# Four blocks on x without its 1/rms, key searches held back once, products given precedence, and a last block in two halves of tokens

## The chip, the cores and the metric

The kernel runs on one core of one Trainium2 chip. The metric is the device time of one execution in microseconds. Three runs of the kernel before gave 3128.99, 3129.6 and 3132.29 us, so the median is 3129.6.

## The reference, cut to what matters

Two transformer blocks run one after the other on 512 tokens of 1024 features, in float32. What the change touches:

```python
# first block
h = rmsnorm(x, norm1_g)                 # x * rsqrt(mean(x * x) + eps) * g
z = h @ w_in + b_in                     # 42 blocks of 128 columns
glu_val, glu_gate, q, k, v, g_conv, g_attn = split(z)
conv_out = conformer_conv(glu_val, glu_gate, ...)   # 31 taps over time
...
# peer: scores against keys, the best 16 of 128 in each half, then experts
q = (h2 @ w_pq).reshape(B, S, 8, 2, 128)
s_top, i_top = top_k(einsum("bshcd,hcnd->bshcn", q, sub_keys), 16)
...
# second block: swiglu, a mixer with two kinds of attention, swiglu, then
hn = rms_norm(h, ple_norm)
h = h + sigmoid(hn @ ple_w_gate) * (p @ ple_w_proj)
return rms_norm(h, final_norm)
```

## The kernel before, in words

Activations lie transposed: eight tiles of 128 features by 512 tokens, `x[0]` to `x[7]`. A product of a weight matrix with them is cut into blocks of 128 output columns. `block` (L213) loads one block's weights (512 KB for 1024 rows), splits them, and issues for each of the eight tiles the three products of `three` (L208): high half of the weights by high half of the activation, high by low, low by high, which together give float32 accuracy. The split of weights is `split` (L189): a cast on ACT (L190) gives the high half `wh`, a subtraction on DVE (L191) the low half `wl`. `wr`, `wh` and `wl` have three buffers each, so weights come up to three blocks ahead; their loads are issued on SP's queue. All products accumulate in eight PSUM banks (`ps`, L139); a bank is free again when its reader is done.

A norm is applied late where that is possible: the products take x times the gain, and their result is multiplied by 1/rms (`self.rstd`), as in `plain` of the mixer (L1051, the product on DVE at L1055). In the first block it is not so: `block1` (L382) squares x (L403, L404), sums over features with products by a column of ones (`col_mean`, L263), takes the root in small steps on DVE (`rsqrt`, L250), spreads it over 128 partitions by four transposes (`bcast`, L274) and a copy (L282), and only then multiplies x by it (L416) and splits the result into `hs`, which all 42 blocks of `w_in` read. Ahead of these stand eight small projections of the embedding `p` (`project`, L389), each copied by ACT (L395) and stored by a DMA that ACT issues (L396). Between them and block 0 stands also the product of `bias_table` (L340), whose result is stored to `rbd`.

The order of instructions on each engine and queue is made ahead of the run by a planner, which takes the instruction of lowest rank among those that it thinks ready; rank is the order in the program, and `high_priority(n)` puts instructions n places forward. Each engine and queue then works strictly in that order. Beside that the kernel spreads work by hand. `later` puts small pieces with a cost into a queue, and `run` (called by `block` with `self.rate`) takes pieces up to a budget: in block1 3.9 units after each block, at 0.65 for each of the 8 x 31 taps of the convolution (L455), which is six taps a block; in peer 4.5 units, at 1.0 for each search `best_keys` (L670), which has two maxima of eight with their places and one replacement. What is left of the searches after the last query block (`pending`, L702) is taken up in the expert stage at 2.2 units a block. `step` advances generators that stand one block back, and `lanes` with `pace` do the same inside the mixer's blocks.

In peer each of 16 query blocks ends with a product by 1/rms on DVE (L687), after which PE makes the scores (L691). Then x's normalized tiles `hn` are split (L704) and 128 expert blocks of 384 tokens follow (L905).

In the mixer the lanes `chosen` and `decays` run beside the blocks of the keys. `choose` makes scores of 128 queries with products at L1160, and searches their best 256 with L1171 and L1172 on DVE.

`tail` (L1445) makes eight blocks of `ple_w_gate`. Behind each follow a product by 1/rms (L1455), a sigmoid on ACT, a product, a sum into x, a square on ACT and a sum of squares (L300). After the last one come the column sums, the root, the broadcast with its copy, and eight last products (L1465), each stored.

Of the kernel before, what the change touches and what calls it, by code (L numbers as in the profile page):

```python
# [10 lines left out]
F32 = mybir.dt.float32  # L11
BF16 = mybir.dt.bfloat16
F32R = mybir.dt.float32r
# [3 lines left out]
AF = mybir.ActivationFunctionType  # L17
OP = mybir.AluOpType
# [4 lines left out]
S = 512  # L23
D = 1024
KD = D // 128
NT = S // 128
# [7 lines left out]
PH = 8  # L34
# [75 lines left out]
class Build:  # L110
    def __init__(self, ctx, tc, a, out):
# [5 lines left out]
        self.offset = 90  # L117
        self.early, self.soon = 160, 90
        self.pad = 3.0
# [183 lines left out]
    def setup(self):  # L303
# [20 lines left out]
        for i in range(4):  # L324
            s = slice(i * 512, (i + 1) * 512)
            self.load(wp[0][:, s], a["ple_w_proj"][:, s])
            self.split(wp[1][:, s], wp[2][:, s], wp[0][:, s])
        self.embedding = ph, wp
        table = sb.tile([128, -(-(NVEC + NCONST) // 32) * 32], F32, name="table")
        self.vecs, self.consts = table[:, :NVEC], table[:, NVEC:NVEC + NCONST]  # L330
        self.load(self.vecs, a["vecs"])
        self.x = []
        for m in range(KD):
            x = self.t("x", S, KD)
            self.load(x, a["x"][m])
            self.x.append(x)
        self.load(self.consts, a["consts"])
        self.ident = self.cst("ident")
# [43 lines left out]
    def block1(self):  # L382
# [14 lines left out]

        for m in range(3):
            project(m)
        accs = []  # L400
        for m in range(0, KD, 2):
            acc, q = (self.t("sq", S, 8, pool=self.ple) for _ in range(2))
            A.activation(acc, x[m], AF.Square)  # L403
            A.activation(q, x[m + 1], AF.Square)  # L404
            V.tensor_add(acc, acc, q)
            accs.append(acc)
        for m in range(3, 6):
            project(m)
        r = self.rsqrt(self.col_mean(accs, D, 1.0 / D), NT)
        for m in range(6, KD):  # L410
            project(m)
        rstd = self.bcast(r)
        hs = []
        for m in range(KD):
# [4 lines left out]
            hs.append((H, L))  # L419
        self.close_pool()  # L420

        b1 = self.ctx_pool("b1")
        c = lambda dt=F32: self.t("c", S, 26, dt, pool=b1)
        few = b1.tile([128, 128], F32, name="few")
# [7 lines left out]
        def gated(j, dst):  # L432

            A.activation(dst, self.block(a["w_in"][j], KD, hs), AF.Tanh, bias=hb[:, j:j + 1], scale=0.5)

# [3 lines left out]
        def glu(m):  # L439
            pv = self.block(a["w_in"][2 * m], KD, hs)  # L440
            v = self.tmp()
# [40 lines left out]
        kT, vtok = c(), c()  # L482
        qT = [b1.tile([128, 4, S], F32, name=f"q{i}") for i in range(2)]

# [154 lines left out]
    def peer(self, hs):  # L639
# [40 lines left out]
        for j in range(2 * PH):  # L680
            key = self.t("key", NKEY, 4, pool=hn_pool)
            self.load(key, a["keys"][j])
            p = self.block(a["w_peer_q"][j], KD, hs)

# [359 lines left out]
    def mixer(self, hs):  # L1044
# [6 lines left out]
        def plain(j, dst, rest=None):  # L1051
            p = self.block(win[j], KD, hs)

            def scale():
                V.tensor_mul(dst, p, self.rstd)  # L1055
                if rest:
                    rest()

            self.when(scale)
            return dst  # L1060
# [384 lines left out]
    def tail(self, hs):  # L1445
        nc, V, A, a, x = self.nc, self.V, self.A, self.a, self.x
        acc = self.t("acc", S, 2)
        for m in range(KD):
            pr = self.tmp()
            self.load(pr, self.prd[m])  # L1450
            p = self.block(a["ple_w_gate"][m], KD, hs)

            def rest(m=m, p=p, pr=pr):
                g = self.tmp()
                V.tensor_mul(g, p, self.rstd)  # L1455
                A.activation(g, g, AF.Sigmoid)
                V.tensor_mul(g, g, pr)
                V.tensor_add(x[m], x[m], g)
                self.sumsq(m, acc, x[m])

            self.when(rest)
        r = self.rsqrt(self.col_mean([acc], D, 1.0 / D), NT)
        rstd = self.bcast(r)
        for m in range(KD):
# [104 lines left out]
```

## Time and profile before

| what | value |
|---|---|
| median of three runs | 3129.6 us |
| the profiled execution | 3130.86 us |
| its span, first to last instruction | 3129.1 us |
| PE (products) busy | 3073.2 us, 98% |
| PEld (weight loads) busy | 2690.7 us, 86% |
| DVE busy | 2157.2 us, 69% |
| ACT busy | 1333.5 us, 43% |
| POOL busy | 304.1 us, 10% |
| mean granted TensorE clock | 0.992 |

The profile is of one execution. Times in its rows are microseconds from the span's start. A row of the timeline has the start, the duration, the engine, the line, the operation, what is written and read, and how many instructions are merged in it; in brackets stands the idle time of the engine before it and who ended that. PE is TensorE, PEld its weight loads, DVE VectorE, ACT ScalarE, SPq and ACTq the queues of SyncE and ScalarE that issue DMAs. Products are pipelined and their ends are modelled, so PE counts as busy from the first to the last of a dense row of them.

### The profile page before, as it was taken

Reading aid. Unit: us, or ns where it says so; the run is one execution under the profiler, and the core shown is the slowest. Engines: PE = TensorE matmul, PEld = TensorE weight load, DVE = VectorE, ACT = ScalarE, POOL = GpSimd, SP = SyncE. Lnnn points to the kernel's source line nnn. Section 1 sums busy time; section 2 is a strip of 40 time slices with the busy share of each in tenths; the row PEclk is TensorE's granted clock in tenths of the full one; section 3 lists DMA queues with packets and bytes.
Section 4 is the critical chain, followed back from the end, with each engine's and each line's share of the span. In section 5 each row is a group of like instructions: output and inputs, shape, how many; then the busy total and the mean of one; then the engine's idle time right before and its main releaser. Section 6 shows DMA issues by size and latency. Waiting matters only on the chain.

```text
span 3129.1 us, 41898 instructions
## 1 busy us (share of the span) xinstructions
PE 3073.2 (98%) x15557; PEld 2690.7 (86%) x15557; DVE 2157.2 (69%) x4086; ACT 1333.5 (43%) x2330; POOL 304.1 (10%) x266
## 2 busy tenths in 40 slices
PE   8999999999999999999999999999999999999997
PEld 6776678899999999999999988887688877888886
DVE  5998677999667766888888764433977655544435
ACT  4246543347888733333333433223433354332222
POOL 0000000011223233222222000000000000000000
PEclk9999999999999999999999999999999999999999
DMA  6321122266889999999999422233223333322332
GB/s 175 94 79 58 53 94 90 92 206 235 312 308 336 322 370 357 368 354 360 349 361 340 157 98 95 94 119 110 68 85 99 124 114 116 103 96 94 96 99 95
DMA packets 203796, 561.07 MB, mean 179 GB/s; under 512 B 20856, under 2 KB 82552, under 8 KB 200520
## 3 DMA queue, kind: packets, MB, share of 16 engines
q1 hardware_dynamic: 140208, 365.66, 34.2%
q0 software_dynamic: 37008, 134.53, 11.8%
q10 hardware_dynamic: 26376, 58.20, 5.2%
q8 instruction: 122, 2.00, 0.3%
q14 instruction: 82, 0.67, 0.1%
HBM read 494.58 MB, written 64.48 MB: 179 GB/s over the span
## 4 chain that ended last, share of the span: by engine, by line
PE 80%; DVE 14%; DMA 3%; ACT 2%; issue 1%; SPq 0%; ACTq 0%; DVEq 0%
PE ps L211 70%; DVE c L455 3%; DVE wl L191 3%; PE ps L834 2%; PE ps L1204 1%; DMA wr<-in_peer_u_dram 1%; DVE topi L676 1%; PE ps L565 1%; PE ps L527 1%; PE ps L1241 1%; DVE top L675 1%; PE ps L1359 1%; DMA tmp<-in_positions_dram 1%; PE ps L556 1%; DVE tk L745 1%
## 5 line engine op out<-in xcount | busy, mean ns | idle before, releaser
L190 ACT CAST wh<-wr 128x1024 fp32r<-128x1024 f32 (+1 forms) x560 | 584.8, 1044 | 1442.3 <-PE ps L211 784.5
L211 PE MATMUL ps<-hH,wh 128*128 128x512 f32 (+1 forms) x2816 | 1063.9, 378 | 5.9 <-ACT hH L190 2.6
L211 PE MATMUL ps<-hH,wl 128*128 128x512 f32 (+1 forms) x2816 | 1047.7, 372 | 10.0 <-DVE wl L191 9.8
L211 PE MATMUL ps<-hL,wh 128*128 128x512 f32 (+1 forms) x2816 | 1047.1, 372 | 0.3
L191 DVE TENSOR_TENSOR wl<-wr,wh 128x1024 fp32r<-128x1024 f32 (+1 forms) x560 | 679.6, 1214 | 338.6 <-ACT wh L190 308.1
L211 PEld LDWEIGHTS ps<-hH,wl 128*128 128x128 f32 x2816 | 531.0, 189 | 87.1 <-DVE wl L191 14.5
L211 PEld LDWEIGHTS ps<-hH,wh 128*128 128x128 f32 x2816 | 530.9, 189 | 83.9 <-issue 6.8
L211 PEld LDWEIGHTS ps<-hL,wh 128*128 128x128 f32 x2816 | 531.8, 189 | 72.9 <-issue 2.6
L211 PE MATMUL ps<-aH,wl 128*128 128x384 f32 (+1 forms) x1376 | 479.0, 348 | 0.0
L211 PE MATMUL ps<-aH,wh 128*128 128x384 f32 (+1 forms) x1376 | 478.9, 348 | 0.0
L211 PE MATMUL ps<-aL,wh 128*128 128x384 f32 (+1 forms) x1376 | 478.9, 348 | 0.0
L211 PEld LDWEIGHTS ps<-aL,wh 128*128 128x128 f32 x1376 | 258.3, 188 | 13.8
L211 PEld LDWEIGHTS ps<-aH,wl 128*128 128x128 f32 x1376 | 258.3, 188 | 13.7
L211 PEld LDWEIGHTS ps<-aH,wh 128*128 128x128 f32 x1376 | 258.3, 188 | 13.6
L860 POOL DMA_INDIRECT row<-in_peer_rows_dram,rows x128 | 161.2, 1259 | 1081.3 <-DVE tk L745 664.7
L860 POOL DMA_INDIRECT row<-in_peer_v_dram,rows x128 | 139.8, 1092 | 354.0 <-DVE acct L872 339.6
L455 DVE SCALAR_TENSOR_TENSOR c<-up,cw,c 128x512 f32<-128x512 f32 x240 | 171.4, 744 | 0.5
L872 DVE SCALAR_TENSOR_TENSOR acct<-row,dots,acct 128x1024 f32<-128x1024 f32 x127 | 162.3, 1278 | 0.0
L865 DVE CUSTOM_DVE_ANT_0 row<-row,htok 128x1024 f32<-128x1024 f32 x128 | 154.5, 1219 | 9.2 <-DMA row<-in_peer_rows_dram,rows 7.3
L211 PE MATMUL ps<-c,wh 128*128 128x512 f32 x384 | 126.2, 409 | 0.0
L1017 DVE TENSOR_TENSOR tmp<-ps,rstd 128x512 f32<-128x512 f32 x44 | 30.4, 691 | 129.8 <-PE ps L211 129.8
L821 DVE TENSOR_TENSOR ohr<-table,trip 128x512 f32<-128x512 f32 x96 | 65.1, 689 | 77.3 <-PE ps L834 73.3
(315 smaller groups left out, 2964.8 us busy)
## 6 DMA issues: line engine op xcount, KB each, us to landing
wr<-in_peer_u_dram SPq DMA_DIRECT2D x128, 512.0 KB
wr<-in_peer_v_dram SPq DMA_DIRECT2D x128, 512.0 KB
wr<-in_ffn_w_in_dram SPq DMA_DIRECT2D x88, 512.0 KB
gd<-tmp ACTq DMA_DIRECT2D x128, 192.0 KB
wd<-wb ACTq DMA_DIRECT2D x24, 1024.0 KB
g<-gd SPq DMA_DIRECT2D x128, 192.0 KB
wr<-in_mix_w_in_dram SPq DMA_DIRECT2D x46, 512.0 KB
wr<-in_w_in_dram SPq DMA_DIRECT2D x42, 512.0 KB
```

Source lines behind the costliest of these rows:

```text
L190: self.A.copy(H, src)
L191: return self.V.tensor_sub(L, src, H.bitcast(F32)).ins
L211: self.T.matmul(ps, l, r, start=first and i == 0, stop=last and i == 2)
L455: V.scalar_tensor_tensor(y, u[:, w:w + S], cw[:, i:i + 1], y, op0=OP.mult, op1=OP.add)
L527: T.matmul(pq[:, j * nk:(j + 1) * nk], qT[ga][P, i * 2 + j, tok], kT[P, k0:k0 + nk], start=True, stop=True)
L556: T.transpose(pt[:, i * 128:i * 128 + 128], sc[i // 2][:, o:o + 128], self.ident)
L565: T.matmul(po[P, :], vtok[:, kb + kv * 64:kb + kv * 64 + 64], pTs[b], start=b == 0, stop=b == nb - 1)
L821: V.tensor_tensor(r4, iota[:, None, :].to_broadcast([128, 4, 128]), trip[:, 128 + o:132 + o, None].to_broadcast([128, 4, 128]), op=OP.is_e ...
L834: T.matmul(pw[:, k * 128:k * 128 + 128], l4[:, k], r4[:, k], start=True, stop=True)
L860: G.indirect_dma_start(out=g, out_offset=None, in_=table, in_offset=bass.IndirectOffsetOnAxis(ap=rows[:, i * NF + j:i * NF + j + 1], axis=0))
L865: V.tensor_tensor_reduce(out=g, in0=g, in1=htok, scale=1.0, scalar=0.0, op0=OP.mult, op1=OP.add, accum_out=dots[:, j:j + 1])
L872: V.scalar_tensor_tensor(acct, g, dots[:, j:j + 1], acct, op0=OP.mult, op1=OP.add)
```

## The change

It has five parts.

1. The projections all come first. The weights of block 0 of `w_in` are loaded and split in `setup`, ahead of `vecs` and `x`. The tiles of x times the gain, without 1/rms, are split into high and low halves `raw` (60 places forward); high halves lie in the tiles that later hold the queries, low halves in tiles of the attention's scores. Blocks 0 to 3 multiply `raw`, and `first_block` multiplies their results by 1/rms; blocks from 4 on use `hs` as before. The constants are loaded after block 0. Squares use the buffers `tmp`, of which there are seven, in place of eight of their own. As blocks 2 and 3 are made before the taps are queued, they no longer carry any.
2. In peer `self.rate` is set to 0 ahead of the last query block.
3. In the mixer the product L1055 gets 40 places of precedence.
4. In the tail the last block is made in two halves of 256 tokens, with the steps behind it on each half, and its squares lie in a tile of their own that the column sums read beside the sum of the others.
5. The last products read the broadcast in PSUM, without the copy.

```diff
--- before.py
+++ after.py
@@ -115,7 +115,7 @@
         self.waiting, self.rstd = None, None
         self.lanes, self.credit, self.budget = [], 0, 0.8
         self.offset = 90
-        self.early, self.soon = 160, 90
+        self.early, self.soon, self.first = 160, 90, 60
         self.pad = 3.0
 
         self.on_act = lambda t: (0, 1) if t == 2 else (0, 1, 2)
@@ -326,6 +326,9 @@
             self.load(wp[0][:, s], a["ple_w_proj"][:, s])
             self.split(wp[1][:, s], wp[2][:, s], wp[0][:, s])
         self.embedding = ph, wp
+        keep, self.offset = self.offset, 0
+        self.first_weights = self.weights(a["w_in"][0], KD)
+        self.offset = keep
         table = sb.tile([128, -(-(NVEC + NCONST) // 32) * 32], F32, name="table")
         self.vecs, self.consts = table[:, :NVEC], table[:, NVEC:NVEC + NCONST]
         self.load(self.vecs, a["vecs"])
@@ -334,7 +337,6 @@
             x = self.t("x", S, KD)
             self.load(x, a["x"][m])
             self.x.append(x)
-        self.load(self.consts, a["consts"])
         self.ident = self.cst("ident")
 
     def bias_table(self):
@@ -395,21 +397,38 @@
             A.copy(r, p)
             nc.scalar.dma_start(self.prd[m], r)
 
-        for m in range(3):
+        for m in range(KD):
             project(m)
+        self.close_pool()
+
+        b1 = self.ctx_pool("b1")
+        c = lambda dt=F32: self.t("c", S, 26, dt, pool=b1)
+        quad = lambda i, dt=F32: b1.tile([128, 4, S], dt, name=f"q{i}", tag=f"q{i}", bufs=1)
+
+
+        high = [quad(i, F32R) for i in range(2)]
+        raw = []
+        with self.tc.high_priority(self.first):
+            for m in range(KD):
+                H = high[m // 4][:, m % 4, :]
+                L = self.t("sc", S, 6, F32R, pool=b1) if m < 6 else self.t("acc", S, 2, F32R)
+                A.activation(H, x[m], AF.Copy, scale=self.vec("norm1_g", m))
+                V.scalar_tensor_tensor(L, x[m], self.vec("norm1_g", m), H.bitcast(F32), op0=OP.mult, op1=OP.subtract)
+                raw.append((H, L))
+        ahead = [self.ps()]
+        for k in range(KD):
+            self.three(ahead[0], self.first_weights[k], raw[k], k == 0, k == KD - 1)
+        self.load(self.consts, a["consts"])
         accs = []
         for m in range(0, KD, 2):
-            acc, q = (self.t("sq", S, 8, pool=self.ple) for _ in range(2))
+            acc, q = self.tmp(), self.tmp()
             A.activation(acc, x[m], AF.Square)
             A.activation(q, x[m + 1], AF.Square)
             V.tensor_add(acc, acc, q)
             accs.append(acc)
-        for m in range(3, 6):
-            project(m)
-        r = self.rsqrt(self.col_mean(accs, D, 1.0 / D), NT)
-        for m in range(6, KD):
-            project(m)
-        rstd = self.bcast(r)
+        mean = self.col_mean(accs, D, 1.0 / D)
+        ahead.append(self.block(a["w_in"][1], KD, raw))
+        rstd = self.bcast(self.rsqrt(mean, NT))
         hs = []
         for m in range(KD):
             h = self.tmp()
@@ -417,10 +436,16 @@
             H, L = self.t("hH", S, 8, F32R), self.t("hL", S, 8, F32R)
             self.split(H, L, h)
             hs.append((H, L))
-        self.close_pool()
-
-        b1 = self.ctx_pool("b1")
-        c = lambda dt=F32: self.t("c", S, 26, dt, pool=b1)
+        ahead += [self.block(a["w_in"][j], KD, raw) for j in range(2, 4)]
+
+        def first_block(j):
+
+            if not ahead:
+                return self.block(a["w_in"][j], KD, hs)
+            r = self.tmp()
+            V.tensor_mul(r, ahead.pop(0), rstd)
+            return r
+
         few = b1.tile([128, 128], F32, name="few")
         hb, lnb, lng, sink = few[:, 0:42], few[:, 42:50], few[:, 50:58], few[:, 58:74]
         V.tensor_scalar(hb, self.vecs[:, VCOL["b_in"]:VCOL["b_in"] + 42], 0.5, None, op0=OP.mult)
@@ -431,13 +456,13 @@
 
         def gated(j, dst):
 
-            A.activation(dst, self.block(a["w_in"][j], KD, hs), AF.Tanh, bias=hb[:, j:j + 1], scale=0.5)
+            A.activation(dst, first_block(j), AF.Tanh, bias=hb[:, j:j + 1], scale=0.5)
 
 
         ys = []
 
         def glu(m):
-            pv = self.block(a["w_in"][2 * m], KD, hs)
+            pv = first_block(2 * m)
             v = self.tmp()
             A.activation(v, pv, AF.Identity, bias=hb[:, 2 * m:2 * m + 1], scale=0.5)
             th = self.tmp()
@@ -480,7 +505,7 @@
             self.start(rest())
 
         kT, vtok = c(), c()
-        qT = [b1.tile([128, 4, S], F32, name=f"q{i}") for i in range(2)]
+        qT = [quad(i) for i in range(2)]
 
         def value():
             pv = self.block(a["w_in"][17], KD, hs)
@@ -680,6 +705,8 @@
         for j in range(2 * PH):
             key = self.t("key", NKEY, 4, pool=hn_pool)
             self.load(key, a["keys"][j])
+            if j == 2 * PH - 1:
+                self.rate = 0
             p = self.block(a["w_peer_q"][j], KD, hs)
 
             def rest(j=j, p=p, key=key):
@@ -1052,7 +1079,8 @@
             p = self.block(win[j], KD, hs)
 
             def scale():
-                V.tensor_mul(dst, p, self.rstd)
+                with self.tc.high_priority(self.o2):
+                    V.tensor_mul(dst, p, self.rstd)
                 if rest:
                     rest()
 
@@ -1444,23 +1472,35 @@
 
     def tail(self, hs):
         nc, V, A, a, x = self.nc, self.V, self.A, self.a, self.x
-        acc = self.t("acc", S, 2)
+        acc, own = self.t("acc", S, 2), self.t("acc", S, 2)
+
+        def rest(m, p, pr, o):
+            g = self.tmp()[:, o]
+            V.tensor_mul(g, p, self.rstd[:, o])
+            A.activation(g, g, AF.Sigmoid)
+            V.tensor_mul(g, g, pr[:, o])
+            V.tensor_add(x[m][:, o], x[m][:, o], g)
+            if m < KD - 1:
+                self.sumsq(m, acc, x[m])
+            else:
+                A.activation(own[:, o], x[m][:, o], AF.Square)
+
         for m in range(KD):
             pr = self.tmp()
             self.load(pr, self.prd[m])
-            p = self.block(a["ple_w_gate"][m], KD, hs)
-
-            def rest(m=m, p=p, pr=pr):
-                g = self.tmp()
-                V.tensor_mul(g, p, self.rstd)
-                A.activation(g, g, AF.Sigmoid)
-                V.tensor_mul(g, g, pr)
-                V.tensor_add(x[m], x[m], g)
-                self.sumsq(m, acc, x[m])
-
-            self.when(rest)
-        r = self.rsqrt(self.col_mean([acc], D, 1.0 / D), NT)
-        rstd = self.bcast(r)
+            if m < KD - 1:
+                p = self.block(a["ple_w_gate"][m], KD, hs)
+                self.when(lambda m=m, p=p, pr=pr: rest(m, p, pr, slice(0, S)))
+            else:
+
+                parts = self.weights(a["ple_w_gate"][m], KD)
+                for o in (slice(0, S // 2), slice(S // 2, S)):
+                    p = self.ps()[:, :S // 2]
+                    for k in range(KD):
+                        self.three(p, parts[k], [y[:, o] for y in hs[k]], k == 0, k == KD - 1)
+                    rest(m, p, pr, o)
+                self.step()
+        rstd = self.bcast(self.rsqrt(self.col_mean([acc, own], D, 1.0 / D), NT), False)
         for m in range(KD):
             V.scalar_tensor_tensor(x[m], x[m], self.vec("final_norm_2", m), rstd, op0=OP.mult, op1=OP.mult)
             nc.sync.dma_start(self.out[m], x[m])
```

## Rows read from the trace of the kernel before

**Rows 1.** The page's first part: busy time, share of the span and instructions of each engine.
```profile
PE 3073.2 (98%) x15557; PEld 2690.7 (86%) x15557; DVE 2157.2 (69%) x4086; ACT 1333.5 (43%) x2330; POOL 304.1 (10%) x266
```

**Rows 2.** PE's waits: who waited for whom, us in total, times, longest.
```profile
PE ps L211 <- DVE wl L191: 9.8, 9, 2.7
PE ps L691 <- DVE tmp L687: 7.2, 2, 4.9
PE ps L268 <- DVE acc L300: 4.3, 1, 4.3
...
PE ps L1160 <- DVE c L1055: 3.4, 1, 3.4
```

**Rows 3.** Stretches: length; PE, PEld, DVE, ACT, POOL busy (count); clock, DMA share, GB/s.
```profile
22.40:32.64 10.24, 7.19 (x16) 4.11 (x17) 9.60 (x19) 6.38 (x12) 0.00 (x0) 0.50 0.75 228
40.00:60.00 20.00, 19.40 (x83) 15.11 (x81) 4.59 (x6) 7.78 (x9) 0.00 (x0) 1.00 0.57 116
60.00:200.00 140.00, 133.76 (x569) 106.20 (x570) 139.89 (x215) 40.57 (x50) 0.00 (x0) 0.99 0.29 90
63.36:66.78 3.42, 3.42 (x10) 2.66 (x9) 3.42 (x9) 0.00 (x0) 0.00 (x0) 0.50 0.51 153
606.08:612.91 6.83, 6.03 (x24) 6.03 (x25) 6.83 (x25) 1.76 (x3) 0.00 (x0) 0.50 0.16 58
1500.00:1700.00 200.00, 200.00 (x1156) 200.00 (x1155) 165.67 (x197) 70.22 (x97) 55.61 (x52) 1.00 0.98 354
2213.76:2220.59 6.83, 5.27 (x10) 2.82 (x10) 6.80 (x20) 0.49 (x1) 0.00 (x0) 0.50 0.49 154
2800.00:3000.00 200.00, 200.00 (x884) 165.62 (x883) 85.93 (x101) 57.57 (x71) 0.00 (x0) 1.00 0.29 95
```

**Rows 4.** Timeline of the first 33 us: PE and two DMA queues.
```profile
17.91 0.33 SPq L178 DMA_DIRECT2D cw<-in_conv_w_dram  x1
18.41 2.96 PE L268 MATMUL ps<-misc,sq 128*128 128x1 f32 x26
...
24.32 1.47 ACTq L396 DMA_DIRECT2D prd<-tmp  x2
...
27.93 1.22 PE L211 MATMUL ps<-hH,wh 128*128 128x512 f32 x2 [0.65 <-ACT hH L190]
...
32.72 0.40 PE L211 MATMUL ps<-hL,wh 128*128 128x512 f32 x1
```

**Rows 5.** The tile hL: low halves; ns min/median/max, first and last start.
```profile
L291 DVE SCALAR_TENSOR_TENSOR hL<-x,table,hH x32: 743/745/749, 460.8 to 3067.3; 128x512 fp32r<-128x512 f32 x32
```

**Rows 6.** Timeline around peer's last query block: DVE and PE.
```profile
600.55 0.47 DVE L675 MAX8 top<-scores 128x8 f32<-128x128 f32 x2
...
606.16 0.67 DVE L687 TENSOR_TENSOR tmp<-ps,rstd 128x512 f32<-128x512 f32 x1
...
612.98 0.34 PE L211 MATMUL ps<-hH,wl 128*128 128x384 f32 x1
```

**Rows 7.** Timeline of the mixer: DVE.
```profile
2214.59 0.67 DVE L1055 TENSOR_TENSOR c<-ps,rstd 128x512 f32<-128x512 f32 x1
```

**Rows 8.** Lines L455 and L592: ns min/median/max, first and last start.
```profile
L455 DVE SCALAR_TENSOR_TENSOR c<-up,cw,c x240: 721/745/754, 46.9 to 334.8; 128x512 f32<-128x512 f32 x120
L592 PE MATMUL ps<-c,onesd x16: 590/592/594, 356.4 to 366.3; 128*128 128x512 f32 x16
```

**Rows 9.** Timeline of the tail, and durations that its steps are priced by.
```profile
3114.56 1.60 PE L268 MATMUL ps<-misc,acc 128*128 128x1 f32 x8 [4.34 <-DVE acc L300]
3119.75 0.59 ACT L282 COPY rstd<-ps 128x512 f32<-128x512 f32 x1 [5.97 <-PE ps L278]
3120.37 5.39 DVE L1465 SCALAR_TENSOR_TENSOR x<-x,table,rstd 128x512 f32<-128x512 f32 x8 [1.82 <-ACT rstd L282]
...
2225.80 0.28 DVE L1168 TENSOR_TENSOR c<-c,table 128x128 f32<-128x128 f32 x1
...
L1316 DVE SCALAR_TENSOR_TENSOR c<-c,table,ps x8: 737/743/748, 2340.0 to 2494.6; 128x512 f32<-128x512 f32 x8
```

## The prediction

> **What bounds the kernel now.** First the page's busy times: PE is busy 98% of the span and DVE 69% [rows 1]. PE is the bound, and the span less its busy time leaves 56 us, so an edit pays only where it takes an idle or slowed stretch from PE. Second, PE's own waits, by who ended them [rows 2]: four are what this change aims at. 9.8 us go to low halves of weights (DVE), 7.2 us to the product in front of the key scores in peer, 4.3 us to the last sum of squares in the tail, 3.4 us to a product L1055 in the mixer. [...]
>
> **Part A, the start.** Before, block 0 waits for the whole chain of 1/rms. The projections end and the column sums run from 18.41 to 21.37, then come the root, its broadcast and the split, and block 0 starts at 27.93 at the slow clock [rows 4]. Ten of its products have started by 32.72, where the full pace begins; at full pace block 0 would have started at 32.72 - 10 x 0.226 = 30.5. What PE has to do in between is the column sums (3.0), the broadcast and the bias product: of the 7.19 us that it is busy in the slow stretch [rows 3], 4.7 lie behind 27.93, so these two took 2.5, or 1.2 at full clock. 18.4 + 3.0 + 1.2 = 22.6 would have been possible: 7.9 us are lost.
>
> After, block 0 needs x only. The eight high halves are written into the first tiles of pool b1, which I take to lie where the pool of the projections lay: cw, also of b1, is loaded at 17.91, just ahead of the projections' end [rows 4]. So the halves begin at about 17.9, not when x lands, and that also hides that x lands later behind the 512 KB that are put ahead of it on SP. From there DVE sets the pace: eight low halves like those of L291, 0.745 us each [rows 5], are 6.0 us; with 0.75 us for the first high half, taken like L291, and 1.2 us for one weight split between them, the last one stands at 25.9, and block 0 ends near 26.4. PE has 24 x 0.226 = 5.4 us of products and the 3.0 us of column sums for these 8.5 us, so the sums fill its gaps. With broadcast and bias product that is 27.6, against 30.5 + 5.4 = 35.9 before: 8.3 us. Moved with it are loads: w_in's first 512 KB go ahead of vecs and x, the 577 KB of consts behind; later weights come three buffers ahead as now. What may hold the high halves is ACT's queue, which also issues the eight projection stores: two of them hold it from 24.32 to 25.79 [rows 4]. With tmp slots now shared by squares and stores I expect some of this to remain. Bounds: 8.3 gained; or the high halves begin only behind that row, at 25.8, so that block 0 ends 8.5 us later at 34.3 and all is done at 35.5, and a slow stretch takes 2.4 more (half of 4.7): 2.0 lost. I take **5.0**, nearer to the gain because all of block 0 leaves the chain.
>
> The price is work: eight high halves on ACT, and on DVE eight low halves (6.0) and four products with 1/rms (4 x 0.69 = 2.8, as L1055's 0.67): 8.8 us. From 60 to 200 DVE is full (139.89 of 140), but from 40 to 60 it has 4.59 us of work in 20 [rows 3], and most of the new work lies before 45. I cost it at **0** by this cover. Without it every us turns into waits for low halves of weights: 8.8 lost. The other end: if the earlier start removes the longest such wait (2.7, [rows 2]) with its slow stretch (3.42 / 2), 4.4 gained.
>
> **Part B, key searches.** Before, four searches run from 600.55 on DVE, then two low halves, and the last query block's product follows at 606.16 [rows 6], though its block ended on PE at about 601.2; PE stops 4.9 us [rows 2], and the next stage runs slow until 612.98 [rows 6]. With the rate at 0 the product runs at 601.3 and its scores at 602.0, right behind the previous ones. Scores and transposes take 0.9 us each at full clock, so the expert stage starts at 603.9 and its ninth product at 603.9 + 8 x 0.173 = 605.3, where before it was at 612.98: 7.7 us. What is late next are the eight low halves of hn on DVE, but they take less than the three products (0.52) that each one feeds. A search that is still in front costs up to 1.4 us (606.16 - 600.55 = 5.6, by 4). The four searches move into the expert stage, where DVE has gaps (165.67 of 200 us in a stretch of its second half, [rows 3]) and PE is bound by its own products; the row fetches on POOL start two blocks later, which nothing on PE waits for. I take **7.0**, bounds 4 to 7.7.
>
> **Part C, the mixer.** L1160 waits 3.4 us [rows 2] for a product of L1055 that frees its PSUM bank, and which ran at 2214.59 behind searches and scans of other lanes [rows 7]; then 5.27 us of PE work run at half clock [rows 3], so 2.6 us more. All of it is 6.0 us. With precedence the product goes ahead of up to 40 instructions. Queued behind it on DVE are the searches and scans, which may now wait for PE's block; PE does not need them for another 40 us. Bounds 0 (the next wait takes over) and 6.0; I take **4.5**, near the upper end, since the product is 0.67 us and all in front of it is other lanes' work.
>
> **Part D, the tail.** PE's last block ends, then 4.34 us pass until the column sums, which take 1.60; a copy of 0.59 stands between broadcast and the eight last products [rows 9]. By halves the block has 48 products of 256 columns; from 0.226 and 0.173 a line gives 0.120, so 5.8 us against 5.4: 0.35 lost. The chain of six steps on 256 columns: an addition of 128 columns takes 0.28, one of 512 0.69, so 0.42 between [rows 9]; the last addition falls away. That is about 5 x 0.42 + 0.25 = 2.35: 2.0 gained. The column sums double in number, but those of the first half's tokens can run ahead: at best half of the 1.60, I take 0.4. The copy goes: 0.6 gained. The last products read the broadcast in PSUM: L1316 does that in 0.743 [rows 9], while L291, of the same kind and size, takes 0.745 from SBUF [rows 5], so nothing is lost there. [...] Sum **2.6**, bounds 1.5 and 3.2.
>
> **Sum.** 5.0 + 0 + 7.0 + 4.5 + 2.6 = 19.1 us. The profiled execution took 3130.9 (span 3129.1 and 1.8 around it), 1.3 above the median of the runs. 3130.9 - 19.1 = 3111.8 for it; against the median 3110.5.
>
> **Rivals.**
> 1. The start gives nothing: ACT, held by its stores, writes the high halves late. For it: the row at 24.32. Against: block 0 no longer needs the root. Then 14.1 us remain: 3115.5. Chance 0.15.
> 2. In the mixer only the name of the wait changes: DVE is full there, and L1160 waits for the next bank. Against: the row names the product alone. 3115.0. Chance 0.12.
> 3. The searches stay in front. The order of each queue comes from a planner, and searches that are ready may be put there even with lower rank. Against: the last product is traced before them. 3110.5 + 7 = 3117.5. Chance 0.06.
> 4. Slower: the convolution taps come late. Blocks 2 and 3 no longer carry taps, so 12 (8.9 us at 0.745) move to the final flush. The last tap now ends at 335.5 and PE's mean over the channels, which needs all, starts at 356.4 [rows 8]: 20.9 us of slack. Less 5 (PE is earlier), 8.9 and 8.8 of new DVE work it is 1.8 us short if no idle time of DVE is used. Each us of lateness there is a us of PE, and a slow stretch follows. It is slower than before only from some 19 us of lateness on; against it stand the 15 us that DVE has idle from 40 to 60. At 24 us of lateness the time would be 3135. Chance 0.05.
>
> **How the numbers follow.** My case has the remaining 0.62. With all bounds at their best (8.3 + 4.4 + 7.7 + 6.0 + 3.2 = 29.6) the time is 3100.0; with all at their worst it is 5 us slower than before. The first three rivals lie at 3115 to 3118, inside 3102 to 3122, which leaves out the very best corner, rival 4, and rivals that come together with lost DVE cover. A change within 0.2% (6.3 us), about what measurement of this kernel can tell from none, needs over 3123.3: 0.05. Slower by more than that: rival 4 beyond its point, 0.04. Faster: 0.91.
>
> **What would show it.** A: block 0's products from 18 to 19 at full clock, column sums between them, no slow stretch from 22.4; a wrong step A shows as ACT's high halves after 21. Added DVE work: the sum of PE's waits for wl stays near 9.8 us. B: L687's last product within 1 us of its block, no 0.50 clock behind. C: no wait of L1160 over 1 us. D: the last column sums some 2 us after PE's last block, no copy behind the broadcast. The prediction is wrong if PE's waits for wl grow by more than 8 us, if the mean over the channels waits for taps, or if a stretch at 0.50 stays at two of the three places.

## The result and the profile after

The changed kernel takes 3181.7 us (median of 6 runs, 3176.1 to 3186.1), the kernel before, run beside it, 3129.9: a ratio of 1.0163, with a 95% interval of 1.0150 to 1.0176. It is 52 us slower, where 3110.5 us, 19 less, had been forecast. The profiled execution took 3179.4 us.

The first thing to look at are the stretches, the same two at full clock as in [rows 3] and then those at half clock. The columns are those of [rows 3].

```profile
1500.00:1700.00 200.00, 200.00 (x1139) 200.00 (x1138) 163.73 (x194) 68.94 (x95) 57.29 (x52) 1.00 0.98 353
2800.00:3000.00 200.00, 200.00 (x862) 162.19 (x861) 89.02 (x108) 57.82 (x71) 0.00 (x0) 1.00 0.28 94
33.84:44.08 10.24, 7.41 (x24) 5.90 (x24) 4.29 (x15) 2.05 (x3) 0.00 (x0) 0.50 0.25 93
78.22:91.87 13.65, 4.36 (x13) 3.59 (x14) 13.08 (x23) 6.66 (x9) 0.00 (x0) 0.50 0.36 54
624.35:631.18 6.83, 5.97 (x24) 5.98 (x25) 6.83 (x36) 1.76 (x3) 0.00 (x0) 0.50 0.22 77
2221.78:2232.03 10.25, 10.25 (x22) 6.57 (x21) 4.07 (x8) 10.15 (x15) 0.00 (x0) 0.50 0.00 0
```

In 200 us in which PE never stops and its granted clock is 1.00, it makes 862 products of 512 columns instead of 884, and 1139 of 384 columns instead of 1156. So a product takes 0.2320 us where it took 0.2262, and 0.1756 where it took 0.1730. No edit lies in either stretch. There are some 7,000 products of 512 columns and 6 x 1024 of 384, so an estimate is 7,000 x 5.8 ns + 6,144 x 2.6 ns = 57 us: the loss is in the pace of these products, not in a wait. The page agrees: PE is busy 50.9 us longer than in [rows 1], in a span that is 48.6 longer.

```profile
PE 3124.1 (98%) x15589; PEld 2713.7 (85%) x15589; DVE 2166.7 (68%) x4100; ACT 1338.3 (42%) x2339; POOL 300.9 (9%) x266
```

PE's waits, in the form of [rows 2], show the four that the change aimed at (L691 is now L718):

```profile
PE ps L519 <- ACT tmp L513: 12.9, 1, 12.9
PE ps L718 <- DVE tmp L714: 5.5, 2, 3.1
PE ps L278 <- DVE sm L260: 5.3, 2, 2.8
PE ps L581 <- ACT sc L572: 4.2, 1, 4.2
...
PE ps L211 <- DVE wl L191: 1.6, 4, 0.5
...
PE ps L268 <- ACT acc L1486: 1.3, 1, 1.3
```

Those for low halves (9.8), for the mixer's L1055 (3.4) and for the tail's last square sum (4.3) are gone or small, the one in front of the key scores is only shorter (7.2 to 5.5), and a new one is longer than any single wait before (4.9): 12.9 us for L513, the biased value block, which PE transposes in L519. The timeline of the start shows where it comes from (SP's issue, then DVE, ACT and PE, in order of time):

```profile
19.38 0.49 PE L211 MATMUL ps<-q,wh 128*128 128x512 f32 x1 [0.81 <-ACT q L415]
25.39 0.39 PE L211 MATMUL ps<-q,wl 128*128 128x512 f32 x1
40.89 0.16 DVE L260 SCALAR_TENSOR_TENSOR sm<-sm 128x4 f32<-128x4 f32 x1
56.95 0.76 SPq L178 DMA_DIRECT2D tmp<-in_positions_dram  x1
72.66 0.43 DVE L360 CAST tmp<-tmp 128x512 f32<-128x512 int32 x1 [4.19 <-DMA tmp<-in_positions_dram]
80.59 0.63 ACT L380 ACTIVATE sin<-sin 128x512 f32<-128x512 f32 x1 [11.49 <-DVE sin L379]
86.79 0.67 ACT L513 ACTIVATE tmp<-ps,table 128x512 f32<-128x512 f32 x1
87.51 1.11 PE L519 MATMUL ps<-table,tmp 128*128 128x128 f32 x4 [12.94 <-ACT tmp L513]
```

Block 0 runs from 19.38 to its last product at 25.39, close to the forecast. But the positions, loaded into a scratch buffer that comes free late, are issued at 56.95 and land 15.7 us later; the sine table follows on DVE, ACT stands before the sine for 11.49 us, and L513 is behind it in ACT's fixed order.

### The profile page after: what moved, and what is told of

It is laid out like the page before. It is cut to its first block, busy times and chain, and to the rows that moved or that the text cites. A ratio compares the mean times of both kernels' runs of the same rounds, so it can differ in the third digit from the quotient of the medians.

```text
span 3177.7 us, 42001 instructions
## 1 busy us (share of the span) xinstructions
PE 3124.1 (98%) x15589; PEld 2713.7 (85%) x15589; DVE 2166.7 (68%) x4100; ACT 1338.3 (42%) x2339; POOL 300.9 (9%) x266
## 4 chain that ended last, share of the span: by engine, by line
PE 87%; DVE 8%; ACT 2%; DMA 2%; issue 1%; ACTq 0%; DVEq 0%; SPq 0%
PE ps L211 77%; PE ps L861 3%; DVE wl L191 2%; PE ps L1232 1%; PE ps L552 1%; DVE topi L701 1%; PE ps L590 1%; DMA wr<-in_peer_u_dram 1%; PE ps L1269 1%; DVE top L700 1%; PE ps L268 1%; PE ps L581 1%; PE ps L1387 1%; PE ps L1356 1%; DMA tmp<-in_positions_dram 0%
```

## The experiments

**Where the tiles lie.** The base pool lays its tiles out in the order in which they are first named. The change names the weights' tiles (`wr`, `wh`, `wl`) ahead of the constants' table. Of the tiles that change places only the table is no multiple of 256 bytes: it has 5248 = 20.5 x 256. Before, weights (`wh` at byte 103808 of each partition) and columns (`hH` at 58752) both lay behind it, 45056 = 176 x 256 apart; after, `wh` lies at 43776 and `hH` at 99712: 55936 = 218.5 x 256. These places are worked out from the order and the sizes of the tiles; a trace does not show them. Runs 1 to 4 are the changed kernel with the old places; the kernel before with the new ones; the changed one with unused bytes around the weights; and three parts of the change on the kernel before.

Run 1, the changed kernel with the old places:

```diff
+        table = sb.tile([128, -(-(NVEC + NCONST) // 32) * 32], F32, name="table")
+        self.x = [self.t("x", S, KD) for m in range(KD)]
+        for tag, n, bufs, dt in (("sm", 16, 24, F32), ("rstd", S, 2, F32), ("hH", S, 8, F32R), ("hL", S, 8, F32R)):
+            self.t(tag, n, bufs, dt)
         keep, self.offset = self.offset, 0
         self.first_weights = self.weights(a["w_in"][0], KD)
...
```

> The changed kernel with nothing altered but where its tiles lie in SBUF: table and x, and one unused tile each of sm, rstd, hH and hL, are named before the first weights, so that wr, wh, wl, x, acc, sm, rstd, hH and hL lie at the byte addresses of the kernel before (wh at 103808 in place of 43776). Theory 1 (the places set the pace of the products): the 512-column product goes back from 232.4 to 226.7-227.3 ns and the 384-column one from 176.0 to 173.3-173.7; 6,900 x 5.5 ns and 6,030 x 2.5 ns give back 38 + 15 = 53 us: about 3128 us. Rival (more waits, other order of work, power): the pace stays at 232 and 176 ns and the time at 3180 us.

Measured: 3132.4 us, ratio to before 1.0007 (0.9998 to 1.0017). Its stretch of 512 columns:

```profile
2800.00:3000.00 200.00, 200.00 (x884) 165.62 (x883) 86.00 (x101) 57.54 (x70) 0.00 (x0) 1.00 0.30 95
```

884 again: 49 us come back with nothing altered but places.

Run 2, the kernel before with the new places:

```diff
+        for tag, dt in (("wr", F32), ("wh", F32R), ("wl", F32R)):
+            self.t(tag, 1024, 3, dt)
         table = sb.tile([128, -(-(NVEC + NCONST) // 32) * 32], F32, name="table")
...
+        self.t("acc", S, 2)
         accs = []
```

> The kernel before with nothing altered but the places: one unused tile each of wr, wh, wl (before the table) and acc (before sm), so that the base pool's tiles lie where the changed kernel has them. Theory 1: its products take 232.4 and 176.0 ns and the kernel 3130 + 53 = 3183 us. Rival: 3130 us, 226.7 ns.

Measured: 3170.8 us, ratio 1.0126 (1.0109 to 1.0143), and the slow pace:

```profile
2800.00:3000.00 200.00, 200.00 (x862) 162.15 (x861) 88.49 (x106) 57.70 (x71) 0.00 (x0) 1.00 0.29 94
```

The places alone make this kernel slow too. It loses 40 us, not the 53 expected: PE is busy 49.0 us longer than in [rows 1] (3122.2 us), but the span is only 40.7 longer, so PE idles 8.3 us less (it waits 6.7 us in place of 9.8 for low halves, 5.9 in place of 7.2 ahead of the key scores, 2.9 in place of 3.4 for the mixer's product).

Run 3, 128 unused bytes ahead of the weights and 384 behind them in the changed kernel, which puts `wh` and `hH` 220 x 256 bytes apart:

```diff
+        sb.tile([128, 32], F32, name="pad0")
         keep, self.offset = self.offset, 0
         self.first_weights = self.weights(a["w_in"][0], KD)
         self.offset = keep
+        sb.tile([128, 96], F32, name="pad1")
         table = sb.tile([128, -(-(NVEC + NCONST) // 32) * 32], F32, name="table")
```

> The changed kernel with 128 unused bytes ahead of wr and 384 behind wl: wr, wh and wl start at 384 bytes above a multiple of 512 as in the kernel before (256 in the changed one); the tiles behind them move by 512 and keep their offset. Theory 1a (the offset of the weights in 512 bytes decides): 226.7 ns and about 3128 us. Theory 1b (the distance or the region of the weights, x or hH decides, not the offset): about 232 ns and 3180 us still.

Measured: 3137.6 us, ratio 1.0017 (1.0007 to 1.0027), pace as before:

```profile
2800.00:3000.00 200.00, 200.00 (x885) 165.58 (x884) 86.70 (x102) 59.00 (x72) 0.00 (x0) 1.00 0.31 96
```

So it is not the region: 512 unused bytes bring the 862 products back to 885. The time is what theory 1a (the weights' own offset counts) forecast, but this run cannot tell that offset from the distance to the columns; run 6 can. Runs 5 and 6 move tiles of the kernel before.

Run 5, a gap of 384 bytes between `wr` and `wh` (and 128 behind `wl`), and run 6, one of 384 ahead of everything from the table on:

```diff
                 raw = self.t("wr", 1024, 3)
...
+                if not hasattr(self, "gap"):
+                    self.gap = self.sb.tile([128, 96], F32, name="gap0")
                 H = self.t("wh", 1024, 3, F32R)
...
```

> The kernel before with 384 unused bytes between wr and wh and 128 behind wl: wh and wl start 256 bytes above a multiple of 512, the raw weights wr and all other tiles stay at 384. Theory 1c (what counts is where TensorE reads its weights, wh and wl): 232 ns for 512 columns, 176 for 384, about 3170 us as in the kernel before with all new places. Rival 1d (what counts is where the raw weights land, or the traffic into wr): 226.7 ns, 3130 us.

```diff
+        sb.tile([128, 96], F32, name="gap")
         table = sb.tile([128, -(-(NVEC + NCONST) // 32) * 32], F32, name="table")
```

> The kernel before with 384 unused bytes ahead of the table: every tile behind it, weights (wr, wh, wl) and columns (x, hH, hL, aH, aL) alike, starts 256 bytes above a multiple of 512, and their distances stay as they were. Theory 1e (the offset of the weights against the columns that are read beside them counts): 226.7 ns, 3130 us. Theory 1f (256 in itself is a bad offset for the weights): 232 ns and about 3170 us, or more if the columns suffer too.

Measured: 3174.3 us (two runs; ratio 1.0141, 1.0121 to 1.0162) for run 5, 3130.7 (1.0000, 0.9989 to 1.0010) for run 6. First the stretch of run 5, then that of run 6:

```profile
2800.00:3000.00 200.00, 200.00 (x863) 162.11 (x862) 88.27 (x105) 57.18 (x70) 0.00 (x0) 1.00 0.29 94
```

```profile
2800.00:3000.00 200.00, 200.00 (x884) 165.65 (x883) 86.37 (x102) 58.26 (x72) 0.00 (x0) 1.00 0.31 95
```

In both runs `wh` lies at the same byte, 104192; in run 6 the columns moved along with it. Moving what PE reads as weights against what it reads as columns costs the pace here (863 products in place of 884); moving both together costs nothing (884). Where `wr` lies, which only DMA, ACT and DVE touch, does not explain it: in run 2 it moved with the weights, in run 5 it stayed with the columns, and both are slow (862 and 863); no run moved `wr` alone. `x` and the other tiles behind the table always moved with `hH` and `hL`, so that the partner of the weights is the columns, and not another of these tiles, is concluded from what PE reads and not shown by itself. Runs 9 to 11 are run 5 with another gap, one run each and so without an interval: 256 bytes; 64 bytes; and 128 bytes between `wh` and `wl`, so that `wl` alone is off.

> The kernel before with 256 unused bytes between wr and wh (and 256 behind wl): the weights' offset against the columns is 256 bytes in 512, where it was 0 in the fast kernels and 384 in the slow ones. If only a distance that is a multiple of 512 is free of cost: pace 232 ns, about 3172 us. If multiples of 256 are enough: 226.7 ns, 3131 us.

> The same with 64 bytes between wr and wh (448 behind wl): offset 64. If only multiples of 256 or 512 are free: about 232 ns and 3172 us, or, if the cost grows with the offset's own alignment, more. If multiples of 64 are enough: 226.7 ns, 3131 us.

> The kernel before with 128 unused bytes between wh and wl: wh and the columns keep their distance, wl alone lies 128 off. Theory 1g (the product that slows is the one during which misplaced weights are being loaded): the products run in turns of hH by wh, hL by wh, hH by wl; wl is loaded while hL by wh runs, so one product in three, hL by wh, goes to some 232 ns and the others stay at 226.7: a third of 49 us, about 3131 + 16 = 3147 us. Theory 1h (the product that reads the misplaced weights is slow): hH by wl at 232, the same total. Rival (any misplaced tile slows all): 3172 us.

Measured: 3127.8, 3175.7 and 3167.5 us, beside 3131.2 for the kernel before. The stretch of run 9 (256 bytes), then of run 10 (64 bytes):

```profile
2800.00:3000.00 200.00, 200.00 (x884) 165.68 (x883) 86.10 (x101) 58.47 (x71) 0.00 (x0) 1.00 0.30 95
```

```profile
2800.00:3000.00 200.00, 200.00 (x858) 161.61 (x857) 87.91 (x104) 57.17 (x70) 0.00 (x0) 1.00 0.29 92
```

Shifting the weights by 256 bytes is free (884 products), by 64 or 384 it is not (858 and 863). For run 11 the groups of lines in the same stretch show the products apart (busy time, mean ns of one), and below them stands one of the kernel before, where all three have 389:

```profile
L216 PE MATMUL ps<-hH,wl 128*128 128x512 f32 x259 | 102.8, 397 | 0.0
L216 PE MATMUL ps<-hL,wh 128*128 128x512 f32 x258 | 102.2, 396 | 0.0
L216 PE MATMUL ps<-hH,wh 128*128 128x512 f32 x258 | 100.4, 389 | 0.0
```

```profile
L211 PE MATMUL ps<-hH,wl 128*128 128x512 f32 x215 | 83.6, 389 | 0.0
```

Two of three are slow: the one during which `wl` is loaded (hL by wh, 396 ns; it and the load of `wl` both start at 2850.69) and the one that uses it (hH by wl, 397 ns), during which the well placed `wh` is loaded again (both start at 2850.92). Both theories of run 11 named one product only and are half right; why the second is slow stays open. In the stage of 384 columns of the same run (1000 to 1700 us) it is not the same two: from start to start `aH` by `wl` takes 175.9 ns and `aH` by `wh` 177.7, but `aL` by `wh` 173.0 (before, all three 173.2 to 173.5).

**The parts.** Run 4, the change without its start, on the kernel before:

```diff
+            if j == 2 * PH - 1:
+                self.rate = 0
...
+                with self.tc.high_priority(self.o2):
+                    V.tensor_mul(dst, p, self.rstd)
```

and the new `tail`, as in the change.

> The kernel before with three of the change's four parts: no key searches in the last query block, precedence for the mixer's products, last block by halves without the copy; the start, and with it all places, as before. By the prediction's terms 7.0 + 4.5 + 2.6 = 14.1 us less: 3115.5 us; by what the trace of the changed kernel shows (a wait of 3.3 us and half clock after the searches still there, half clock in the mixer still there) 3 to 8 us less: 3122 to 3127. Theory 1: pace 226.7 ns. Rival (one of these three makes the products slow): 232 ns, about 3170 us.

Measured: 3124.7 us, ratio 0.9978 (0.9969 to 0.9988): 6.3 us less than before, inside what the after trace had led to, under half of the prediction's 14.1. Its waits and its timeline of DVE around the last query block (L689 is L687 of before):

```profile
PE ps L211 <- DVE wl L191: 9.7, 10, 3.3
PE ps L693 <- DVE tmp L689: 6.0, 2, 3.7
...
PE ps L1163 <- DVE c L1058: 3.4, 1, 3.4
```

```profile
597.85 0.69 DVE L689 TENSOR_TENSOR tmp<-ps,rstd 128x512 f32<-128x512 f32 x1
...
602.82 0.56 DVE L191 TENSOR_TENSOR hL<-hn,hH 128x384 fp32r<-128x384 f32 x1
603.27 0.10 DVE L676 MATCH_VALUE_LOAD topi<-top,scores 128x8 f32 x1
...
604.27 0.57 DVE L191 TENSOR_TENSOR hL<-hn,hH 128x384 fp32r<-128x384 f32 x1
604.73 0.70 DVE L689 TENSOR_TENSOR tmp<-ps,rstd 128x512 f32<-128x512 f32 x1
```

Before, four searches and two low halves stood in front of the product [rows 6]; now it is seven low halves, with pieces of two older searches between them, and it comes 6.9 us after the product before it, where in the kernel before it came 7.3 after (598.83 to 606.16). Run 8 gave that product precedence:

```diff
                 q = self.tmp()
-                V.tensor_mul(q, p, self.rstd)
+                with self.tc.high_priority(self.o2 if j == 2 * PH - 1 else 0):
+                    V.tensor_mul(q, p, self.rstd)
```

> The three parts on the kernel before (3124.7 us), and the scaling of the last query block by 1 / rms given precedence on VectorE. With the three parts alone it ran at 604.73 us, behind seven subtractions of the next stage's low halves (0.56 us each) and pieces of the older searches, 6.88 us after the scaling before it, and TensorE waited 3.82 us and ran 3.4 us at half clock. Theory B (it is these low halves that now stand in front, not the last block's searches): the scaling runs some 3 to 4 us earlier, the wait falls below 1 us: 3.8 - 1 + 1.7 = 4.5 us less, 3120 us. Rival (the scaling waits for its product, or the low halves behind it then hold the next stage's first products by as much): 3124.7 within 1 us.

Measured: 3124.2 us (ratio 0.9980, 0.9970 to 0.9990), the same as run 4. The timeline of DVE shows that the product still stands behind seven low halves (the last one is shown):

```profile
599.17 0.69 DVE L690 TENSOR_TENSOR tmp<-ps,rstd 128x512 f32<-128x512 f32 x1
...
605.59 0.57 DVE L191 TENSOR_TENSOR hL<-hn,hH 128x384 fp32r<-128x384 f32 x1
606.05 0.71 DVE L690 TENSOR_TENSOR tmp<-ps,rstd 128x512 f32<-128x512 f32 x1
```

So the time went as the rival said, but theory B was not put to the test: the product did not move. What the stage would be with it in front is open.

Run 7 is run 1 with the positions loaded early. Run 12 is run 4 with the same, in `self.t("acc", S, 2, I32)` in place of `c(I32)`:

```diff
         self.load(self.consts, a["consts"])
+        p = a["positions"]
+        self.positions = c(I32)
+        self.load(self.positions, bass.AP(tensor=p.tensor, offset=p.offset, ap=[[0, 128], [1, S]]))
...
-        pi = self.tmp(I32)
-        p = self.a["positions"]
-        self.load(pi, bass.AP(tensor=p.tensor, offset=p.offset, ap=[[0, 128], [1, S]]))
+        pi = self.positions
```

> The changed kernel with the old places, and the load of the positions issued early, into a buffer of its own, right behind the constants (some 21 us) and not at 54 us into a scratch buffer that comes free late. In the changed kernel with old places TensorE idled 16.9 us ahead of the value's transposes at 71.1 us and then ran 17.1 us at half clock. Theory A (the start's gain was lost because the positions landed at 73 us, beside the 1.5 MB store of the bias rows, and ScalarE waited for the sine in front of the value's copy): this idle time and half of the half-clock stretch go, 16.9 + 8.5 = 25 us in that execution, 10 + 5 = 15 in one with the shorter wait, of which some 3 to 5 come back as waits for low halves of weights as in the kernel before: 3132 - 12 = about 3120 us, range 3114 to 3125. Rival (the ScalarE order or the late first low halves keep it): within 3 us of 3132.

> The three parts on the kernel before (3124.7 us), with the positions loaded at the start into a buffer of their own (the acc pair's, unused until later; hH to wl move up by 4096 bytes, their distances stay). In the kernel before VectorE waited 12.1 us for the positions until 59.8 us, and the sine and cosine tables then stood in front of low halves of weights, for which TensorE waited 2.8 and 3.5 us at 59 to 71 us, before 3.4 us of half clock. If these waits come from the late positions: 6.3 + 1.7 = 8 us less at best, some 5 us with what is late next: 3119 to 3121 us. If the waits come from weights that arrive late themselves: 3124.7 within 1.5.

Measured: run 7 3126.1 us (ratio 0.9987, 0.9978 to 0.9997), 6.3 less than run 1, outside the expected 3114 to 3125: late positions cost time, but half of what was expected. Run 12 3114.2 us (0.9949, 0.9932 to 0.9966), 10.4 less than run 4, twice the 5 expected, and 17 less than the kernel before: the fastest of all. PE's waits of run 7, then of run 12:

```profile
PE ps L278 <- DVE sm L260: 5.5, 2, 3.0
...
PE ps L520 <- ACT tmp L514: 3.5, 1, 3.5
```

```profile
PE ps L694 <- DVE tmp L690: 6.0, 2, 3.7
PE ps L1164 <- DVE c L1059: 3.4, 1, 3.4
...
PE ps L211 <- DVE wl L191: 2.9, 7, 0.7
```

In run 12 the waits for low halves go from 9.7 to 2.9 us, as the tables' arithmetic on DVE, which started at 59.43 in run 4, starts at 41.69 and is done by 54.4, and from 60 to 200 PE is never idle (133.76 of 140 us in [rows 3]):

```profile
60.00:200.00 140.00, 140.00 (x611) 112.69 (x609) 139.60 (x225) 45.43 (x73) 0.00 (x0) 1.00 0.29 90
```

## Why the prediction was wrong

**The step that failed** stands before Part A: "an edit pays only where it takes an idle or slowed stretch from PE". It took 0.226 us a product as given, 200 us over the 884 of [rows 3], and 0.173 for 384 columns, over the 1156 there; the sum had no term for what the change does to it, 5.8 ns on each product of 512 columns and 2.6 on each of 384. Part A did see that weights are loaded ahead of x; it read that as an order of loads alone, and not as an order of naming that moves tiles. Run 1 puts this term at 49 us (3181.7 against 3132.4), and without it the kernel is no faster than before (ratio 1.0007), not 19 us faster: the rest of the sum was wrong too. The prediction's own sign shows that as well: a stretch at 0.50 stays at all three places (from 33.84, 624.35 and 2221.78). Stage by stage in the profiled executions (us between the first start of L691, the last of L971, the first of L1241, the last of L1359 and the end, by the lines of before):

| kernel | start to keys | keys, experts | mixer | its end | to the end | span |
|---|---|---|---|---|---|---|
| before | 511.5 | 1262.3 | 518.9 | 323.6 | 512.8 | 3129.1 |
| after | 530.2 | 1271.7 | 529.0 | 324.8 | 521.9 | 3177.7 |
| run 1: old places | 524.9 | 1258.4 | 519.1 | 323.7 | 509.7 | 3135.8 |
| run 4: no new start | 509.7 | 1259.0 | 518.5 | 323.7 | 509.7 | 3120.6 |
| run 7: run 1, positions early | 512.3 | 1258.8 | 518.5 | 323.7 | 509.7 | 3123.0 |
| run 12: run 4, positions early | 501.6 | 1258.0 | 518.9 | 323.8 | 509.7 | 3112.0 |

**Part A** (5.0 gained) is a loss of 7.8 us, run 1 less run 4 by their medians (run 1's profiled execution, in the table, lies 5.1 us above its median). Its timing of block 0 was right to the microsecond, and ACT's stores did not hold the high halves. What failed is "With broadcast and bias product that is 27.6", as the changed kernel's timeline shows (PE, DVE, PE):

```profile
31.82 3.69 PE L268 MATMUL ps<-misc,tmp 128*128 128x1 f32 x26
38.97 1.23 DVE L191 TENSOR_TENSOR wl<-wr,wh 128x1024 fp32r<-128x1024 f32 x1 [2.07 <-ACT wh L190]
41.11 1.11 PE L278 MATMUL ps<-table,sm 128*128 128x128 f32 x4 [2.83 <-DVE sm L260]
```

The squares stood behind the high halves on ACT, so the column sums came late; the clock fell to 0.50 at 33.84 while PE made them, though its last stop (1.1 us) had ended at 26.87; the root's steps on DVE were broken off for 3.2 us (36.90 to 40.11) by a split of weights that waited for ACT; and PE stopped 2.8 us ahead of the broadcast. Starts of PE's n-th product of 512 columns, counted in the traces (the projections make the first 48), show the lead given back:

| n | 50 | 100 | 150 | 200 | 300 |
|---|---|---|---|---|---|
| before | 28.5 | 42.0 | 54.8 | 72.8 | 96.8 |
| run 1 | 19.3 | 40.0 | 53.5 | 67.5 | 111.0 |
| run 7 | 19.6 | 41.2 | 54.4 | 68.4 | 97.8 |
| run 12 | 28.6 | 41.5 | 54.9 | 66.3 | 90.3 |

Nine us at 50 are 1 to 2 at 100 and 150. The price of the added DVE work was rightly near 0 (waits for wl fell to 1.6 us); but no step followed the load of the positions, which the old start issued at 42.67 and this one at 56.95, and whose lateness costs PE 17 us in run 1 (9.5 in run 3, 12.9 in the changed kernel, where 13.65 us at 0.50, from 78.22 to 91.87, reach past it). Late positions are not the whole of it: with the positions early in both, the new start is still 11.9 us slower than the old one (run 7 against run 12), 10.7 of them ahead of the keys in the table. Run 7 has lost its lead over run 12 by n = 100 and is 7.5 us behind at 300; 3.5 us of the wait for the value block are still there, and what makes up the rest was not tried. Rival 1, that the start gives nothing, came nearest to Part A, for another reason than ACT's stores.

**Part B** (7.0, bounds 4 to 7.7) gave 3.3 (1262.3 less 1259.0). Its step "With the rate at 0 the product runs at 601.3" failed. In run 4 the 5.2 us ahead of the product (599.57 to 604.73) hold seven low halves of hn, 3.2 us from start to start, and pieces of two older searches, 2.0 us. The eight low halves, named there as what is late next, were weighed against the products that they feed and not against the query product that they now precede, and the 5.6 us by which it priced four searches held two of them. Rival 3, that searches stay in front, came true in part.

**Part C** (4.5, bounds 0 to 6.0) gave nothing that shows: 518.5 against 518.9, the wait of 3.4 us still there in run 4. Precedence did not bring the product forward, as it did not in run 8: it starts 6.0 us after the one before it (2203.61 to 2209.63), with searches and scans in front, where it started 4.9 after (2209.70 to 2214.59). In the changed kernel the wait is gone, but 10.25 us at half clock stand in the same stage; with the old places the stage takes 519.1, and the wait is back, as PE's waits of run 1 show:

```profile
PE ps L519 <- ACT tmp L513: 16.7, 1, 16.7
...
PE ps L1188 <- DVE c L1083: 3.5, 1, 3.5
```

The time is that of rival 2, but run 4 does not show its mechanism, another wait in place of this one. The 10.25 us follow no stop: PE is busy through all 10.28 us before 2221.78, at a granted clock of 1.00, some 6 of them with products of L1188 and L1151, which use 64 and 16 of the 128 rows. The prediction charges half clock only behind a stop; that does not hold here.

**Part D** (2.6, bounds 1.5 to 3.2) gave 3.1 (512.8 less 509.7), and its steps are seen in the changed kernel's timeline:

```profile
3162.06 1.17 PE L268 MATMUL ps<-misc,acc 128*128 128x1 f32 x10
3164.55 0.83 PE L268 MATMUL ps<-misc,acc 128*128 128x1 f32 x6 [1.32 <-ACT acc L1486]
...
3168.96 5.36 DVE L1505 SCALAR_TENSOR_TENSOR x<-x,table,ps 128x512 f32<-128x512 f32 x8 [1.21 <-PE ps L278]
```

The last column sums start 2.5 us after PE's last block has ended (3162.06; some 2 were forecast), and the eight products that read the broadcast in PSUM take 5.36 us, against 5.39 from SBUF [rows 9]: the read from PSUM cost nothing that this trace shows.

Rival 4 did not come: no wait of the mean over the channels is among PE's. But its slack went from 20.9 to 5.9 us: in the changed kernel the last tap ends at 369.8 and the mean starts at 375.7. The parts as measured, 7.8 - 6.3 + 49 = 51 us, add up to nearly the 52 of the result; as each is a difference between two of the runs, this says only that the runs agree.

## What to carry to other kernels

Read the pace of the products, count per 200 us in a stretch where PE never stops, before looking for waits: here 862 products in place of 884 pointed to the 49 us that came back in run 1, and no row of PE's waits did. When an edit names a tile earlier or adds one, look at where the others went, and keep the distance between the tiles that TensorE reads as weights and as columns at a multiple of 256 bytes, the only distances that cost nothing here (884 or 885 products in 200 us, against 858 to 863 at 176.25, 177.5 and 218.5 x 256); 512 unused bytes around the weights did it in run 3 (885). When work is moved to the front of a start, follow every small load and every table behind it to its new issue time: the fastest version (run 12, 3114.2 us) keeps the old start and, beside the three other parts, only loads the positions early.

## What the runs showed of the hardware that had not been expected

TensorE's products of 512 columns take 0.226 us when `wh` and `wl` lie a multiple of 256 bytes from the columns (distances of 176, 177 and 220 x 256 tried), and 0.232 to 0.233 at 176.25, 177.5 and 218.5 x 256; products of 384 columns go from 0.1730 to 0.176. The granted clock is 1.00 in both, and the region (run 3, 885 products in 200 us) and an offset that both share (run 6, 884) do not count. The slow places cost 1.2% (run 11) to 1.6% (the changed kernel) of the whole time. The products of 256 columns in the new tail lose nothing: from start to start 118.7 ns in the changed kernel and 119.8 to 119.9 in the others, in 47 intervals each. Why the distance counts was not tried.

In the changed kernel the clock falls to 0.50 in two places where PE had not just stopped: at 33.84, while it makes 26 column sums of one column, and at 2221.78, behind products that use 64 and 16 rows. Why it falls there was not tried.
